# A gate stage's transposes go from TensorE to the DMA, by way of DRAM and as 16-bit halves

## The chip, the cores and the metric

The program runs on one core of one Trainium2 chip. A core has TensorE (PE in the profile; matmuls, and the only engine that could transpose in the kernel before), VectorE (DVE), ScalarE (ACT), GpSimd (POOL), a sync engine (SP) which here only issues DMAs, and 16 DMA engines that all queues share. Each engine executes its instructions in order, so an instruction that waits holds up everything behind it on its engine, and a DMA that waits on SP holds up every DMA behind it on SP. The metric is the device time of one execution in microseconds. The kernel before takes 794.83 us in the median of 3 runs (793.85 to 795.38).

## The reference, cut to what matters

One layer of a trunk, on 512 tokens of width 2048, all in float32:

```python
hn = rmsnorm(x, norm_g[i])
y = swa_mixer(hn, swa_w_in[j], swa_w_out[j], swa_sinks[j], rel_bias)   # ends in (out * silu(gate)) @ w_out
x = x + y
emb = p[i] @ ple_proj[i]
g = jax.nn.sigmoid(rmsnorm(x, ple_norm[i]) @ ple_gate[i])
x = x + emb * g
return rmsnorm(x, final_g)
```

What matters here is the seam between two products: `@ w_out` (the out stage) makes y with tokens on the partitions, x + y is formed in that layout, and `rmsnorm(x) @ ple_gate` (the gate stage) needs x + y once more with its columns on the partitions. Somewhere 512 x 2048 floats have to be transposed.

## The kernel before, in words

Activations of a product are the stationary-side forms with columns on the partitions; weights stream past. To keep float32 accuracy, every float32 operand is split into a high and a low fp32r part, and every product is three matmuls (`mm3`, L124 to L128): high times high, low times high, high times low. Each piece of weights (128 x 1024 floats, 512 KB) is loaded by an SP DMA (L720), cast to its high part by ACT (L727) and subtracted to its low part by DVE (L728).

Each of the two last weighted stages multiplies 2 x 2 blocks by a Winograd scheme, with seven block products instead of eight. The products are numbered 1 to 7; a tuple (`ORDER_OUT`, `ORDER_PLE`) sets the order in which they run. A product has two halves (jj = 0 and 1, the two 512-wide column blocks of its result) of four steps each; a step is one piece of weights and 12 matmuls. In the out stage product 2 is itself done by a smaller Winograd scheme, whose 14 small pieces (6 matmuls each) are put between the steps by the tables `SMALL` and `small_steps`. So the out stage has 62 pieces, numbered 0 to 61, and the gate stage's first product starts with piece 62.

`Forms.steps` makes the four stationary forms of a product: a sum of blocks on DVE where there is one, then a cast on ACT and a subtraction on DVE for each. The blocks of the gate stage are halves of `hT[j]`, the transposed columns 512j to 512j+511 of x + y: product 2 needs columns 1024 to 2047 of the first 256 tokens, product 7 the columns 0 to 1023 of all tokens.

x + y is summed in SBUF as `x1[j][:, t]` (column block j of 512, token block t of 128; 16 tiles) by DVE (`add_to_x`, L1031 and L1033), as the products of the out stage come out of PSUM. When a tile is complete, ACT sums its squares (`squares`, L1001). Then `turn` (L1015) transposes it on TensorE, two column chunks by two token blocks at a time, into a PSUM bank, and ACT copies it out and scales it by the norm's gain (L1018). Of the 16 such turns, 12 stand in the last product of the out stage and 4 in the first product of the gate stage.

What sets the order. The program text sets the order on TensorE and SP throughout. On DVE, ACT and POOL a scheduler sets it from the start of the out stage up to the second product of the gate stage; from there on the program text does. Pieces are prepared ahead: the SP load is placed up to 6 pieces ahead of the piece's use in the out stage (L703 to L720, a ring of 8 buffers from the third product on) and the split two pieces ahead, with three buffers for split pieces, so that ACT can split piece n only when TensorE has finished piece n-3. Products 7, 6 and 4 of the gate stage use weights that are grown in place: loaded once, then another block is added by an accumulating POOL DMA (L707).

The embedding's input `pT` is loaded and split (L1160 to L1162) between the two stages and used from the third product of the gate stage on.

Of the kernel before, what the change touches and what calls it, by code (L numbers as in the profile page):

```python
# [11 lines left out]
F32 = mybir.dt.float32  # L12
F32R = mybir.dt.float32r
AF = mybir.ActivationFunctionType
# [4 lines left out]
D = 2048  # L19
# [36 lines left out]
def trunk_kernel(ctx: ExitStack, tc: tile.TileContext, a: dict):  # L56
# [587 lines left out]
    def blk(t):  # L644
# [4 lines left out]
    ORDER_OUT, ORDER_PLE = (1, 7, 6, 5, 3, 4), (2, 7, 1, 6, 5, 3, 4)  # L649

    SMALL = {
        (5, 0): {1: 1, 3: 1}, (5, 1): {1: 7, 3: 7}, (3, 0): {1: 6, 3: 6}, (3, 1): {1: 2, 3: 2},
        (4, 0): {0: 5, 1: 5, 2: 4, 3: 4}, (4, 1): {0: 3, 1: 3},
# [151 lines left out]
    far_from, far_to = at_out[6, 0][0], at_ple[ORDER_PLE[0], 0][0]  # L805

    class Forms:
# [6 lines left out]
        def steps(self, p):  # L814

            self.made[p] = []
            for h in range(2):
# [3 lines left out]
                if self.nm == "o":  # L821
                    src, sub = {
                        1: (a11, None), 7: (a11, (a21, a11)), 2: (a12, None), 6: (a11, (a22, a11)),
# [7 lines left out]
                if sub:  # L831
                    nc.vector.tensor_sub(src, *sub)
                    yield
# [116 lines left out]
    fg = late.tile([P, D], F32, name="fg")  # L950
    pTh = late.tile([P, 2, S], F32R, name="pTh")
    pTl = late.tile([P, 2, S], F32R, name="pTl")
# [5 lines left out]
    def banks(p, jj, nm):  # L958

        if p in (6, 5, 3):  # L960
            return chain[jj]
        tag = ("to" if p in (7, 2) else "sp")[jj]
        ps = [bank(f"{nm}{p}_{jj}_{tb}", tag) for tb in range(2)]
        if p == 1:
            chain[jj] = ps
        return ps

    later = []
# [6 lines left out]
    def unit(p, jj, at, forms, todo, between=lambda m: None):  # L975

        ps = banks(p, jj, forms.nm)
        f = forms.made[p]
        first = p not in (6, 5, 3)
        for m in range(4):  # L980
            bh, bl = B.get(at[p, jj][m])
            for kk in range(2):
# [22 lines left out]
    def turn(kp, th, tag):  # L1005

        g = kp // 2
        if g not in hT:
            hT[g] = quarter(f"hT{g}")
        tp = bank(f"tp{kp}_{th}", tag)  # L1010
        for n in range(2):
            k = 2 * kp + n
            for tb in range(2):
                src = x1[k // 4][:, 2 * th + tb, (k % 4) * P : (k % 4 + 1) * P]
                nc.tensor.transpose(tp[:, (2 * n + tb) * P : (2 * n + tb + 1) * P], src, ident)  # L1015
        for n in range(2):
            k = 2 * kp + n
            nc.scalar.mul(hT[g][:, k % 4, th * 256 : th * 256 + 256], tp[:, n * 256 : n * 256 + 256], pn[:, k : k + 1])  # L1018

    ple_forms = Forms(hT, "g")  # L1020
    ple_first = ple_forms.steps(2)


    missing = {(j, t): {(0, 0): 1, (1, 0): 3, (0, 1): 1, (1, 1): 2}[t // 2, j // 2] for j in range(4) for t in range(NB)}
# [3 lines left out]
    def add_to_x(j, t, sign, ps):  # L1028
# [6 lines left out]
        if not missing[j, t]:  # L1035
            squares(t, j)

# [4 lines left out]
    small_forms = {}  # L1042

    def small_form(q):
# [5 lines left out]
        fh, fl = (  # L1050
            acts.tile([P, 2, 256], F32R, tag=tag, name=f"small_{tag}{q}").rearrange("p k (h t) -> p (k h) t", h=2)
            for tag in ("ah", "al")
        )
# [16 lines left out]
        (6, 1, 2): 1, (5, 0, 0): 7, (5, 0, 2): 7, (5, 1, 0): 6, (5, 1, 2): 6, (3, 0, 2): 2, (3, 1, 0): 5, (3, 1, 2): 5,  # L1070
        (3, 1, 3): 4, (4, 0, 1): 3, (4, 0, 3): 3,
# [26 lines left out]
    def add_y(p, jj, tb, ps):  # L1098
        c11, c12, c21, c22 = ((2 * v + jj, 2 * u + tb) for u in range(2) for v in range(2))
        whither = {  # L1100
            1: [(c11, -1)], 7: [(c22, 1), (c21, -1)], 6: [(c21, -1)], 5: [(c22, 1)], 3: [(c12, 1)],
# [5 lines left out]
    turns = []  # L1107


# [3 lines left out]
    waiting = {(7, 0): (1, 0), (6, 0): (1, 1)}  # L1113
    held = {}
    for n, p in enumerate(ORDER_OUT):
        nxt = out_forms.steps(ORDER_OUT[n + 1]) if n < 5 else iter(())
        for jj in range(2):
# [11 lines left out]
            def todo():  # L1129
# [5 lines left out]
                if p == 4:  # L1135

                    for _ in range({0: 1, 1: 2, 2: 2, 3: 2, 5: 1, 6: 2, 7: 2}.get(4 * jj + step, 0)):
                        turn(*turns.pop(0), "o")
                    if jj:
                        next(ple_first, None)  # L1140
# [8 lines left out]
        if p == 3:  # L1149
            nc.sync.dma_start(fg, a["final_g"].partition_broadcast(P))  # L1150
        if p == 3:
# [308 lines left out]
```

## Time and profile before

| | us |
|---|---|
| median of 3 runs | 794.83 |
| profiled execution, own time | 794.82 |
| its span | 793.1 |
| out stage, first to last matmul start | 452.3 to 606.4 |
| gate stage, first matmul start | 607.4 |
| TensorE transposes, first to last start | 574.8 to 620.1 |
| busy TensorE / VectorE / ScalarE / GpSimd | 783.2 / 585.7 / 506.7 / 148.5 |

A row of a group of instructions names line, engine, operation, output and inputs, count, and busy time or durations; a row of a stretch gives each engine's busy time in it. Neighbouring matmuls overlap in the profile (each lasts longer than the distance to the next), so what a matmul costs is read from the distance of starts or from the chain of work that ended last, not from its duration. The profiled execution's time is 1.7 us above its span.

### The profile page before, as it was taken

Reading aid. Unit: us, or ns where it says so; the run is one execution under the profiler, and the core shown is the slowest. Engines: PE = TensorE matmul, PEld = TensorE weight load, DVE = VectorE, ACT = ScalarE, POOL = GpSimd, SP = SyncE. Lnnn points to the kernel's source line nnn. Section 1 sums busy time; section 2 is a strip of 40 time slices with the busy share of each in tenths; the row PEclk is TensorE's granted clock in tenths of the full one; section 3 lists DMA queues with packets and bytes.
Section 4 is the critical chain, followed back from the end, with each engine's and each line's share of the span. In section 5 each row is a group of like instructions: output and inputs, shape, how many; then the busy total and the mean of one; then the engine's idle time right before and its main releaser. Section 6 shows DMA issues by size and latency. Waiting matters only on the chain.

```text
span 793.1 us, 11181 instructions
## 1 busy us (share of the span) xinstructions
PE 783.2 (99%) x3746; PEld 656.0 (83%) x3746; DVE 585.7 (74%) x1155; ACT 506.7 (64%) x1067; POOL 148.5 (19%) x248
## 2 busy tenths in 40 slices
PE   9999999999999999999999999999999999999995
PEld 8888888888888888888888888888888888888885
DVE  4547587867867587767777899778866757988896
ACT  6743576666767586766666654466699656656765
POOL 0200423242413324132324200000000120210000
PEclk9999999999999999999999999999999999999998
DMA  9977999897989989898987498667864996787533
GB/s 349 275 215 264 207 275 303 223 267 215 277 227 269 223 249 258 230 247 235 244 227 182 140 365 337 197 212 232 275 237 142 346 203 202 157 225 220 176 107 106
DMA packets 45066, 185.23 MB, mean 234 GB/s; under 512 B 6656, under 2 KB 7680, under 8 KB 39888
## 3 DMA queue, kind: packets, MB, share of 16 engines
q1 hardware_dynamic: 36928, 143.30, 53.0%
q0 software_dynamic: 8080, 41.22, 27.1%
q8 instruction: 29, 0.48, 0.2%
q14 instruction: 29, 0.24, 0.1%
HBM read 177.63 MB, written 62.97 MB: 303 GB/s over the span
## 4 chain that ended last, share of the span: by engine, by line
PE 99%; DVE 0%; ACT 0%; ACTq 0%; issue 0%; DVEq 0%
PE gps L126 7%; PE gps L127 7%; PE gps L128 7%; PE qps L126 7%; PE qps L127 7%; PE qps L128 7%; PE o L127 6%; PE g L128 6%; PE g L127 5%; PE o L126 5%; PE o L128 5%; PE g L126 5%; PE s L477 2%; PE o L583 2%; PE vps L290 2%; PE pt L541 2%
## 5 line engine op out<-in xcount | busy, mean ns | idle before, releaser
L728 DVE TENSOR_TENSOR blo<-braw,bhi 128x1024 fp32r<-128x1024 f32 x102 | 124.4, 1222 | 40.9 <-ACT bhi L727 40.6
L727 ACT CAST bhi<-braw 128x1024 fp32r<-128x1024 f32 x102 | 107.3, 1052 | 72.2 <-PE o L128 24.8
L126 PE MATMUL gps<-xh,whi 128*128 128x512 f32 x256 | 100.0, 390 | 0.0
L127 PE MATMUL gps<-xl,whi 128*128 128x512 f32 x256 | 99.9, 390 | 0.0
L128 PE MATMUL gps<-xh,wlo 128*128 128x512 f32 x256 | 99.8, 390 | 0.0
L126 PE MATMUL qps<-xh,whi 128*128 128x512 f32 x224 | 87.8, 392 | 0.0
L127 PE MATMUL qps<-xl,whi 128*128 128x512 f32 x224 | 87.4, 390 | 0.0
L128 PE MATMUL qps<-xh,wlo 128*128 128x512 f32 x224 | 87.3, 390 | 0.0
L110 DVE TENSOR_TENSOR wlo<-wraw,whi 128x1024 fp32r<-128x1024 f32 x60 | 73.7, 1229 | 6.1 <-ACT whi L109 5.9
L547 DVE TENSOR_TENSOR r<-pt,r 128x256 fp32r<-128x256 f32 x64 | 27.2, 424 | 66.5 <-ACT r L546 65.6
L546 ACT CAST r<-pt 128x256 fp32r<-128x256 f32 x64 | 23.9, 373 | 80.9 <-PE pt L541 80.8
L126 PE MATMUL g<-bhi,fhg 128*128 128x512 f32 x192 | 75.1, 391 | 0.0
L126 PE MATMUL o<-bhi,fho 128*128 128x512 f32 x192 | 74.8, 390 | 0.0
L128 PE MATMUL g<-bhi,flg 128*128 128x512 f32 x192 | 74.8, 389 | 0.0
L127 PE MATMUL o<-blo,fho 128*128 128x512 f32 x192 | 74.8, 389 | 0.0
L128 PE MATMUL o<-bhi,flo 128*128 128x512 f32 x192 | 74.7, 389 | 0.0
L127 PE MATMUL g<-blo,fhg 128*128 128x512 f32 x192 | 74.7, 389 | 0.0
L557 POOL TENSOR_SCALAR_AFFINE_SELECT own<-r 64x512 fp32r<-64x512 f32 (+1 forms) x48 | 32.5, 677 | 224.6 <-DVE r L547 208.7
L109 ACT CAST whi<-wraw 128x1024 fp32r<-128x1024 f32 x60 | 62.2, 1039 | 5.4 <-issue 4.0
L492 POOL COPY t<-sinkb 128x2 f32<-128x2 f32 x64 | 53.2, 839 | 57.7 <-ACT sinkb L873 32.4
L707 POOL DMA_DIRECT2D grown<-in_ple_gate x16 | 13.8, 861 | 231.0 <-DVE blo L728 226.7
L128 PEld LDWEIGHTS gps<-xh,wlo 128*128 128x128 f32 x256 | 48.1, 188 | 10.3
(228 smaller groups left out, 1800.3 us busy)
## 6 DMA issues: line engine op xcount, KB each, us to landing
wraw<-in_w_gate_in SPq DMA_DIRECT2D x32, 512.0 KB, 6.5
w_out<-in_w_out POOLq DMA_DIRECT2D x32, 512.0 KB, 8.0
braw<-w_out SPq DMA_DIRECT2D x32, 512.0 KB, 4.4
wraw<-in_w_q SPq DMA_DIRECT2D x28, 512.0 KB, 5.3
braw<-in_ple_gate SPq DMA_DIRECT2D x24, 512.0 KB, 4.1
braw<-in_w_out SPq DMA_DIRECT2D x22, 512.0 KB, 4.2
xw<-in_first SPq DMA_DIRECT2D x14, 640.5 KB, 6.4
w_out<-in_w_out SPq DMA_DIRECT2D x16, 512.0 KB, 10.1
```

What stands on the lines that cost most here:

```text
L109: nc.scalar.copy(hi, raw)
L110: nc.vector.tensor_sub(lo, raw, hi.bitcast(F32))
L126: nc.tensor.matmul(ps, sh, mh, start=first, stop=False, skip_group_check=more)
L127: nc.tensor.matmul(ps, sh, ml, start=False, stop=False, skip_group_check=more)
L128: nc.tensor.matmul(ps, sl, mh, start=False, stop=last, skip_group_check=more)
L290: nc.tensor.matmul(v_ps[t], h[:, c], part_of(high_at, 256, 512), start=f, stop=e, skip_group_check=True)
L492: nc.gpsimd.tensor_copy(two(0, W + W - 1 if late else W, 1), sinkb[:, d : d + 1].unsqueeze(1).to_broadcast([P, 2, 1]))
L546: nc.scalar.copy(rh, src)
L547: nc.vector.tensor_sub(rl, src, rh.bitcast(F32))
L557: nc.gpsimd.affine_select(out=flat(own), in_=flat(r).bitcast(F32), pattern=[[0, 8], [sign, HB]], compare_op=ALU.is_ge, fill=0.0, base=-HB ...
L727: nc.scalar.copy(hi, raw)
L728: nc.vector.tensor_sub(lo, raw, hi.bitcast(F32))
```

## The change

The transposes leave TensorE. When a tile of x + y is complete, POOL copies it into a buffer with the two 16-bit halves of each float pulled apart (`apart`, L1029 of the changed kernel), and a POOL DMA stores it to DRAM as 128 tokens x 2 halves x 512 columns (L1030). Some steps later SP issues a transposing DMA (L1045) that reads it as 256 rows (token, half) of 512 16-bit values and writes 512 columns of 256 values into `hT[j]`, where the halves lie side by side again as float32. ACT then scales `hT[j]` in place, in SBUF, for pairs of token blocks (L1040). `cross`, called once a step, places the transposing DMA at the fourth call after the store and the scaling at the third call after the second transposing DMA of a pair; `forward` makes the gate stage's forms as far as their input is scaled.

To give this time, the order of products changes: the out stage runs 1, 7, 4, 6, 5, 3 instead of 1, 7, 6, 5, 3, 4 (product 4 now adds to product 7's PSUM banks, so that the sums into x fall by four), and the gate stage starts with product 7 instead of 2. The small products move with it. Their forms, `pT`'s split and the final gain get other buffers.

```diff
-    ORDER_OUT, ORDER_PLE = (1, 7, 6, 5, 3, 4), (2, 7, 1, 6, 5, 3, 4)
+    ORDER_OUT, ORDER_PLE = (1, 7, 4, 6, 5, 3), (7, 2, 1, 6, 5, 3, 4)
...
-    def turn(kp, th, tag):
...
-                nc.tensor.transpose(tp[:, (2 * n + tb) * P : (2 * n + tb + 1) * P], src, ident)
...
+    def apart(t, j):
...
+        nc.gpsimd.tensor_copy(to, x1[j][:, t, :].bitcast(U16).rearrange("p (c h) -> p h c", h=2))
+        nc.gpsimd.dma_start(halves_of[j][t * P : (t + 1) * P], to)
+        written.append((clock[0], t, j))
+
+    def cross():
+
+        clock[0] += 1
+        while crossed and crossed[0][0] <= clock[0] - 3:
+            _, th, j = crossed.pop(0)
+            for k in range(4):
+                part = hT[j][:, k, th * 256 : th * 256 + 256]
+                nc.scalar.mul(part, part, pn[:, 4 * j + k : 4 * j + k + 1])
+            scaled.add((th, j))
+        while written and written[0][0] <= clock[0] - 4:
+            _, t, j = written.pop(0)
...
+            nc.sync.dma_start_transpose(
+                to[:, :, t * 2 * P : (t + 1) * 2 * P], halves_of[j][t * P : (t + 1) * P].rearrange("t h c -> (t h) c")
+            )
...
         if not missing[j, t]:
             squares(t, j)
+            apart(t, j)
...
-        if p == 3:
-            nc.sync.dma_start(fg, a["final_g"].partition_broadcast(P))
-        if p == 3:
-            turns = [(kp, th) for kp0, th in ((4, 1), (4, 0), (0, 0)) for kp in range(kp0, kp0 + 4)]
-    run(ple_first)
+        if p == 5:
+            due(7)
+            fg = late.tile([P, D], F32, tag="two", name="fg")
+            nc.sync.dma_start(fg, a["final_g"].partition_broadcast(P))
+    finish()
...
     nc.sync.dma_start(pT, a["pT"])
+    pTs = late.tile([P, 2, 2, S], F32R, tag="one", name="pTs")
+    pTh, pTl = pTs[:, 0], pTs[:, 1]
```

Three places show how the instructions stand. First SP, at the seam between the stages, before (`braw62` to `braw68` are weights of the gate stage's first product, by piece number; `pT` is the embedding's input):

```order
L720 DMA braw61_6181<-w_out_4_1_3_808 128x1024 [waits DMAHW3_49,DMASW3_49,DVE_49]
L720 DMA braw62_6258<-in_ple_gate 128x1024 [waits DMAHW4_49]
L720 DMA braw63_6270<-in_ple_gate 128x1024 [waits DMAHW5_49,Pool_49]
L720 DMA braw64_6310<-in_ple_gate 128x1024 [waits DMAHW6_49]
L1160 DMA pT_6352<-in_pT 128x1024 [waits DMAHW7_49]
L720 DMA braw65_6361<-in_ple_gate 128x1024 [waits DMAHW7_49,DMAHW0_49,DVE_49]
```

and the same place now (`halves_of2` and `halves_of3` are the DRAM tensors that the POOL DMAs write; DMASW names a wait for such a DMA):

```order
L721 DMA grown67_6295<-ple_gate_7_1_1_814 128x1024 [waits DMAHW5_49,DVE_49]
L1045 DMA_TRANSPOSE hT2_6139<-halves_of2_5009 128x4x256 [waits DMAHW6_49,DMASW2_49]
L1209 DMA pT_6329<-in_pT 128x1024 [waits DMAHW7_49]
L721 DMA grown68_6339<-ple_gate_7_1_2_815 128x1024 [waits DMAHW0_49,DVE_49]
L1045 DMA_TRANSPOSE hT2_6139<-halves_of2_5009 128x4x256 [waits DMAHW1_49,DMASW3_49]
L721 DMA grown69_6363<-ple_gate_7_1_3_816 128x1024 [waits DMAHW2_49,DVE_49]
L1045 DMA_TRANSPOSE hT3_6210<-halves_of3_5010 128x4x256 [waits DMAHW3_49,DMASW6_49,Activation_49]
L721 DMA braw70_6425<-in_ple_gate 128x1024 [waits DMAHW4_49]
L1045 DMA_TRANSPOSE hT3_6210<-halves_of3_5010 128x4x256 [waits DMAHW5_49,DMASW1_49]
```

The load of `pT` now stands behind a transposing DMA, which waits for a store of a tile that the out stage's last product completes in its first half.

Second ACT, around the start of the gate stage (piece 62), before:

```order
L727 CAST bhi60_6228<-braw60_6144 128x1024 [waits DMAHW2_49,PE_49]
L1161 CAST pTh_5006<-pT_6352 128x1024 [waits DMAHW7_49]
L727 CAST bhi61_6260<-braw61_6181 128x1024 [waits DMAHW3_49,DVE_49,PE_49]
L1018 ACTIVATE hT3_6073<-tp7_0_6247,pn_68 128x256 [waits PE_49]
L1018 ACTIVATE hT3_6073<-tp7_0_6247,pn_68 128x256
L844 CAST fhg2_11_6346<-hT3_6073 128x512 [waits Activation_49]
L727 CAST bhi62_6272<-braw62_6258 128x1024 [waits DMAHW4_49,DVE_49,PE_49]
```

and now, in two pieces, at pieces 63 and 64 and at pieces 68 and 69 (`hT3` are columns 1536 to 2047):

```order
L728 CAST bhi63_6297<-grown63_6192 128x1024 [waits DMAHW7_49,DVE_49,PE_49]
L1212 CAST pTs_6331<-pT_6329 128x1024 [waits DMAHW7_49]
L728 CAST bhi64_6341<-grown64_6212 128x1024 [waits DMAHW1_49,DVE_49,PE_49]
...
L728 CAST bhi68_6427<-grown68_6339 128x1024 [waits DMAHW0_49,PE_49]
L1267 COPY s7_6334<-g7_0_1_6338 128x512
L1040 ACTIVATE hT3_6210<-hT3_6210,pn_68 128x256 [waits DMAHW5_49,DMAHW3_49]
L1040 ACTIVATE hT3_6210<-hT3_6210,pn_68 128x256 x2
L728 CAST bhi69_6464<-grown69_6363 128x1024 [waits DMAHW2_49,DVE_49,PE_49]
```

`pT`'s cast moved from ahead of piece 61's cast to ahead of piece 64's, and a scaling that waits for the last two transposing DMAs stands ahead of piece 69's cast.

Third POOL, which before did nothing in the out stage but load x; now, at the end of the out stage (`apart12` is the buffer of the last four tiles; `grown62` to `grown65` are the accumulating DMAs into the weights of pieces 62 to 65):

```order
L1029 COPY apart12_6233<-x1s_5004 128x1024 [waits DMASW4_49,DMASW6_49,DMASW3_49,DVE_49]
L1029 COPY apart12_6233<-x1s_5004 128x1024 [waits DVE_49]
L1030 DMA halves_of2_5009<-apart12_6233 128x1024 [waits Pool_49] x2
L708 DMA grown62_6169<-in_ple_gate 128x1024 [waits DMAHW5_49,DMAHW6_49,DMAHW3_49,DVE_49]
L708 DMA grown63_6192<-in_ple_gate 128x1024 [waits DMAHW4_49,DMAHW0_49,DMAHW7_49,DMASW5_49,DVE_49]
L1029 COPY apart12_6233<-x1s_5004 128x1024 [waits DVE_49]
L1030 DMA halves_of3_5010<-apart12_6233 128x1024 [waits Pool_49]
L708 DMA grown64_6212<-in_ple_gate 128x1024 [waits DMAHW1_49,DMASW7_49,DVE_49]
L1029 COPY apart12_6233<-x1s_5004 128x1024 [waits DVE_49]
L708 DMA grown65_6242<-in_ple_gate 128x1024 [waits DMAHW3_49,DMASW0_49,DVE_49]
L1030 DMA halves_of3_5010<-apart12_6233 128x1024 [waits DMASW1_49,Pool_49]
```

Both copies of a pair stand ahead of the pair's stores for `halves_of2`, and the last store of `halves_of3` stands behind two accumulating DMAs that wait for VectorE to have split pieces 64 and 65.

129 lines of the change are left out of this document (77 added, 52 removed).

## The prediction

> **What bounds the kernel now.** I read the page first (busy shares, chain), then the waits of TensorE, then the transposes, then the chain around the seam of the two stages.
>
> ```profile
> span 793.1 us, 11181 instructions
> PE 783.2 (99%) x3746; PEld 656.0 (83%) x3746; DVE 585.7 (74%) x1155; ACT 506.7 (64%) x1067; POOL 148.5 (19%) x248
> PE 99%; DVE 0%; ACT 0%; ACTq 0%; issue 0%; DVEq 0%
> PE warm_ps L141 <- PEq L1450: 0.8, 1, 0.8
> ```
>
> The chain that ended last is 99% TensorE, and TensorE's only recorded wait is 0.8 us at the start. So each microsecond taken from TensorE is gained, if nothing takes its place; and each wait that TensorE did not have is lost in full.
>
> What a transpose costs is read from the chain (start, length), since single matmuls overlap:
>
> ```profile
> L1015 PE MATMUL tp<-ident,x1s x64: 270/272/273, 574.8 to 620.1; 128*128 128x128 f32 x64
> L1018 ACT ACTIVATE hT<-tp,pn x32: 458/469/492, 576.6 to 621.3; 128x256 f32<-128x256 f32 x32
> 606.75 0.87 PE tp L1015 x8
> 610.37 0.44 PE tp L1015 x4
> ```
>
> Eight hold TensorE for 0.87 us, four for 0.44: 0.109 us each, not the 0.272 of a single record. All 64 are worth 64 x 0.109 = 7.0 us. More cannot be gained on TensorE, since no other matmul goes.
>
> **A clock for the seam.** Where work must be ready follows from these rows:
>
> ```profile
> 480.00:520.00 40.00, 40.00 (x178) 33.11 (x178) 32.85 (x39) 19.97 (x23) 0.00 (x0) 1.00 0.77 272
> L126 PE MATMUL g<-bhi,fhg x192: 389/389/477, 607.4 to 752.9; 128*128 128x512 f32 x192
> ```
>
> 178 matmuls in 40 us are 0.225 us each, 2.70 us a step of 12. The gate stage started at 607.4 behind 48 transposes; without them (5.2 us) it starts at 602.2 on the same clock. From there, if nothing waits: the last out product's first half ends at 591.4 and its second at 602.2; piece 64 begins at 607.6 and piece 69 at 621.1.
>
> **The change part by part.** *Removed*: 64 transposes, -7.0 us. Four sums into x also go from VectorE, and ACT scales from SBUF instead of PSUM (32 scalings before and after); neither engine was on the path: 0.
>
> *Added, on the path from a tile of x to its form*: POOL's copy, POOL's store, the transposing DMA. No row shows the copy's shape, the store or such a transfer. The nearest:
>
> ```profile
> L557 POOL TENSOR_SCALAR_AFFINE_SELECT own<-r x48: 652/660/1584, 104.7 to 448.9; 64x512 fp32r<-64x512 f32 x24, 128x512 fp32r<-128x512 f32 x24
> L1181 POOL DMA_DIRECT2D x1s<-s x4: 856/860/866, 725.7 to 740.2; - x4
> DMA to landing us min/median/max: 4.0/5.2/5.8
> out<-x1s SPq DMA_DIRECT2D x14, 256.0 KB, 2.8
> braw<-in_ple_gate SPq DMA_DIRECT2D x24, 512.0 KB, 4.1
> pT<-in_pT SPq DMA_DIRECT2D x1, 512.0 KB, 9.6
> ```
>
> The copy has the bytes of a 512-column POOL operation (0.66) and twice its elements (1.32); I take 1.3, since the elements are what POOL loops over. The store (256 KB from POOL) I take at the 5.2 of L1181, which has its size and queue, bounds 2.8 and 5.8. The transposing DMA (256 KB on SP) lies between the 2.8 of a quiet 256 KB store and the 9.6 that `pT` took in a burst; I take 3.5, near plain loads.
>
> [...]
>
> *First wait: `pT`.* SP now issues `pT` behind a transposing DMA that waits for the store of a tile finished by the last product's first half (order rows above). Before, the load stood free:
>
> ```profile
> 583.74 0.70 SPq L1160 DMA_DIRECT2D pT<-in_pT  x1
> 597.04 1.05 ACT L1161 CAST pTh<-pT 128x1024 fp32r<-128x1024 f32 x1
> 598.58 1.22 DVE L1162 TENSOR_TENSOR pTl<-pT,pTh 128x1024 fp32r<-128x1024 f32 x1
> 606.79 1.05 ACT L727 CAST bhi<-braw 128x1024 fp32r<-128x1024 f32 x1 [1.11 <-PE o L128]
> L1031 DVE TENSOR_TENSOR x1s<-o,x1s x16: 679/684/692, 485.5 to 606.8; 128x512 f32<-128x512 f32 x16
> ```
>
> Issued 13 us before its cast, it cost nobody anything, though nothing uses it before the third gate product. Now: TensorE is done at 591.4, drained at 591.6; the two sums (0.68 each) end at 592.3 and 593.0; POOL copies both before it stores either: 594.9; the store lands at 594.9 + 5.2 = 600.1; SP issues the transpose and `pT`, 600.5. `pT` lands 4.1 to 9.6 later; among weights, grown blocks and transposes I take 6: 606.5. Behind it ACT holds piece 64's cast. On VectorE, in order: `pT`'s low part (after the cast, 1.05; then 1.22), a sum into x (0.68), piece 64's low part (1.22): 606.5 + 4.2 = 610.7. TensorE wants it at 607.6 + 0.2. **Wait: 2.9 us.** With the low ends (0.66, 4.0, 4.1) the part is ready at 606.3 and there is none; with the high ends (copies 1.3 plus a block of 1.2 each, 5.8, 9.6) it is ready at 617.5: 9.7.
>
> *Second wait: the last pair.* The scheduler put the scaling of the last two tiles, (columns 1536 to 2047, first 256 tokens), ahead of piece 69's cast on ACT. The sum of the first of these two tiles stands behind `pT`'s low part on VectorE, so it ends at 609.4 although TensorE finished the product at 602.2; the second's behind piece 64's low part, at 611.4. POOL: copy to 610.7, store issued to 611.6 (0.86), accumulating DMA for piece 64 to 612.4, copy to 613.7, the DMA for piece 65 (which waits for that piece's split) to 614.6, then the last store: lands at 614.6 + 5.2 = 619.8, transpose at 623.3. ACT then has three scalings (0.47 each), piece 69's cast 1.05, VectorE the low part 1.22: 627.0. TensorE wants it at 621.1 + 0.2 + 2.9 (already late) = 624.2. **Wait: 2.8 us.** Bounds: with the low ends it is ready at 619.9, no wait; with the high ends some 6.
>
> *Third: VectorE and POOL shut each other out.* This row of a two-element copy is the sign:
>
> ```profile
> L492 POOL COPY t<-sinkb x64: 177/1161/1462, 77.5 to 431.0; 128x2 f32<-128x2 f32 x64
> 302.06 1.34 POOL L492 COPY t<-sinkb 128x2 f32<-128x2 f32 x1
> 302.16 1.22 DVE L110 TENSOR_TENSOR wlo<-wraw,whi 128x1024 fp32r<-128x1024 f32 x1
> L110 DVE TENSOR_TENSOR wlo<-wraw,whi x60: 1217/1219/1755, 58.2 to 436.8; 128x1024 fp32r<-128x1024 f32 x60
> 520.00:560.00 40.00, 40.00 (x178) 33.15 (x177) 31.96 (x36) 24.94 (x35) 0.00 (x0) 1.00 0.72 227
> 560.00:575.00 15.00, 15.00 (x69) 12.38 (x68) 12.96 (x16) 9.49 (x13) 0.00 (x0) 1.00 0.83 284
> 575.00:621.00 46.00, 46.00 (x236) 38.54 (x235) 32.47 (x40) 41.02 (x79) 0.00 (x0) 1.00 0.62 218
> ```
>
> Two elements take POOL 0.18 us or 1.16, the length of VectorE's subtraction beside it; and the subtraction, 1.22 in nearly all of 60, once took 1.76, longer by most of a POOL operation. So 16 copies of 1.3 us may take 21 us from VectorE, busy 77.4 of 101 us here (the three stretches). Wholly added, 98.2 would stand against 94 us: 4.2 late; overlapped with VectorE's sums from PSUM, nothing. I take 1.0, a quarter, since a split has some 3 us of slack (two steps, 5.4, less cast and subtraction, 2.3).
>
> [...]
>
> *Moved for nothing*: the order of products (same matmuls); the final gain's load, now also behind a transpose, not needed before the end of the kernel. SP's weight loads in the out stage run up to ten pieces ahead of TensorE (8 buffers), so a transposing DMA that waits there some microseconds eats only that lead.
>
> *Sum*: 793.1 - 7.0 + 2.9 + 2.8 + 1.0 = 792.8 of span; with the 1.7 us around it (own time 794.82) **794.5 us**, against the median of 794.83: no change.
>
> **The rivals.**
>
> *All is hidden.* With the low ends both waits vanish: 794.8 - 7.0 = 787.8. For it: SP's long lead, two to four steps between store and transpose, DMA queues a quarter to a third idle here (share 0.62 to 0.83). Against: the loads now stand in one line behind data that TensorE has only just made, and `pT` cannot start before.
>
> *The transfers are slow (the slower side).* One mechanism: the transposing DMA or its store lands late, and ACT, in order, holds the casts behind the scalings. Its place is ahead of pieces 64 and 69. A store later by d is paid once in the first wait and again in the second; a transpose later by d in the second, and by its traffic in front of `pT` in the first. With 3 us more for each: 794.5 + 3 + 6 = 803, less where slack remains; I put it at 800 (797 to 804). It decides from d of about 1 us, since some 2 us lead from my sum to slower. For it: `pT`'s 9.6 in a burst, and no row of such a transfer. Against: plain 256 KB stores at 2.8.
>
> *VectorE becomes the bound.* 4.2 us in place of 1.0: 797.7. For it: its 80 to 86% in two of the three stretches. Against: 71% in the last, where the late work is.
>
> **How the numbers follow.** What a measurement of this kernel can tell from no change is about 0.2%, 1.6 us: 793.2 to 796.4. The forecast (the waits take most of the gain, 792 to 797): 0.40, of which 0.10 is faster, 0.23 the same, 0.07 slower. All hidden (787.8 to 792): 0.29. Slow transfers: 0.21. VectorE: 0.10. So faster 0.39, same 0.23, slower 0.38. The forecast's own range is 792 to 797; with both signs holding most of the chance the range is 788.0 to 801.0, from all hidden to beyond the middle of the slow case.
>
> **What would show it.** In the changed kernel's waits: TensorE waiting at pieces 64 and 69 for VectorE's low parts, 2 to 4 us each; on ACT the longest waits at the cast of `pT` (for a DMA) and at the scaling of `hT`; `pT` issued near 600 and not at 584; POOL's copies between 1.3 and 2.5 us, VectorE's subtractions beside them lengthened. If TensorE shows no wait there, all is hidden; if it waits earlier too, ahead of scalings in the out stage, or the transposing DMAs take over 6 us, the transfers are slow. The sum is wrong at its root if matmuls ran slower: the granted clock must stay at 1.00.

## The result, and the profile after

The changed kernel takes 819.43 us in the median (814.71 to 822.23), the kernel before on the same chip 794.53 (793.85 to 795.38): slower by 25 us, ratio 1.031, 95% interval 1.026 to 1.036. 794.5 was forecast, and the range ended at 801.0. All times below leave out three executions that lay over 1.5% above the fastest of their kernel, one each of e5 (826.5), e6 (805.0) and e14 (825.9); with them the three medians would be 815.3, 795.6 and 809.4.

The page of the changed kernel: span, busy times, the chain that ended last.

```profile
span 818.2 us, 11139 instructions
PE 785.0 (96%) x3682; PEld 650.2 (79%) x3682; DVE 587.6 (72%) x1151; ACT 507.4 (62%) x1067; POOL 177.9 (22%) x280
PE 81%; DMA 8%; DVE 4%; issue 3%; ACT 2%; POOL 1%; SPq 1%; DVEq 0%; ACTq 0%; POOLq 0%
```

A chain that was 99% TensorE now runs through DMAs for 8% of the span. TensorE does 64 instructions less and is yet busy 1.8 us longer. Its waits, and ACT's for transposed tiles, from the table of waits (total, times, longest, in us; `o` is the out stage, `g` the gate stage):

```profile
PE g L127 <- ACT bhi L728: 10.9, 2, 6.6
PE o L128 <- DVE blo L729: 5.8, 8, 1.2
PE o L127 <- ACT bhi L728: 4.8, 4, 2.0
PE g L128 <- DVE blo L729: 1.3, 3, 0.5
ACT hT L1040 <- DMA hT<-halves_of: 32.0, 7, 11.0
```

TensorE waits 22.8 us in 17 waits: 12.2 in the gate stage, 10.6 already in the out stage (1.25 of them at 472 and 478 us, before the first tile is copied at 534), each time for a weight piece's cast or low part. ACT, which makes the casts, waited 32 us for transposed tiles. The account: TensorE's idle time rises from 9.9 (793.1 - 783.2) to 33.2 us (818.2 - 785.0), +23.3; the transposes are gone, -7.0; so TensorE should be busy 776.2 us and is busy 785.0, +8.8. Together +25.1, the difference of the spans.

The 8.8 us show in the stretches of the changed kernel (length, then PE, PEld, DVE, ACT, POOL busy, granted clock, DMA share, GB/s):

```profile
615.00:620.00 5.00, 5.00 (x24) 4.14 (x23) 1.55 (x2) 1.45 (x3) 1.62 (x2) 1.00 0.94 249
630.00:635.00 5.00, 4.54 (x10) 3.17 (x11) 4.29 (x10) 4.97 (x9) 2.12 (x3) 0.50 1.00 201
650.00:655.00 5.00, 4.06 (x9) 2.89 (x10) 4.19 (x4) 3.23 (x5) 0.85 (x1) 0.50 0.53 140
```

Behind its two long waits TensorE got half its clock: 19 matmuls in 8.6 us where some 38 fit, about 4.3 us lost. The rest fits the restarts. Before a wait the last matmul runs out its whole 0.39 us, where otherwise the next one starts after 0.23; and after a wait of 0.32 to 1.24 us that no second one follows at once, the second matmul starts some 0.33 us behind the first, not 0.23. By my estimate from these that is about 0.26 for each wait, and 17 x 0.26 = 4.4. One of them, and TensorE's wait for piece 64:

```profile
611.15 0.50 PE L128 MATMUL o<-blo,fho 128*128 128x512 f32 x1 [1.24 <-DVE blo L729]
611.48 0.40 PE L129 MATMUL o<-bhi,flo 128*128 128x512 f32 x1
622.69 0.50 PE L128 MATMUL g<-blo,fhg 128*128 128x512 f32 x1 [0.35 <-DVE blo L729]
```

Where the waits come from shows in ACT's timeline at the seam (start, length, and in brackets the idle time before and its cause):

```profile
618.60 1.05 ACT L1212 CAST pTs<-pT 128x1024 fp32r<-128x1024 f32 x1 [3.55 <-DMA pT<-in_pT]
626.84 0.91 ACT L1040 ACTIVATE hT<-hT,pn 128x256 f32<-128x256 f32 x2 [6.25 <-DMA hT<-halves_of]
648.18 1.30 ACT L1040 ACTIVATE hT<-hT,pn 128x256 f32<-128x256 f32 x3 [10.97 <-DMA hT<-halves_of]
```

and in the chain of the same stretch (start, length):

```profile
614.19 4.38 DMA pT<-in_pT
631.79 7.21 DMA halves_of<-apart
640.68 8.62 DMA braw<-in_ple_gate
```

`pT`, forecast to be issued at 600.5 and to land at 606.5, is issued at 614.19 and lands at 618.57. The gate stage starts at 616.5, 14 us behind the forecast's clock, so that TensorE reaches piece 64 late too and waits only 0.35 us there (row above). The scaling of columns 1024 to 1535 stands ahead of piece 65's cast, that of 1536 to 2047 ahead of piece 69's; behind these two TensorE stands 4.3 and 6.6 us. The transposing DMAs as a group (time that the issue takes on SP, min/median/max in ns, first and last start; then from issue to landing in us):

```profile
L1045 SPq DMA_TRANSPOSE hT<-halves_of x16: 1232/1427/3611, 550.6 to 639.0; - x16
DMA to landing us min/median/max: 3.3/6.1/11.5
```

### The profile page after: what moved, and what is told of

The parts are those of the page before. It is cut to its first block, busy times and chain, and to the rows that moved or that the text cites. A ratio compares the mean times of both kernels' runs of the same rounds, so it can differ in the third digit from the quotient of the medians.

```text
span 818.2 us, 11139 instructions
## 1 busy us (share of the span) xinstructions
PE 785.0 (96%) x3682; PEld 650.2 (79%) x3682; DVE 587.6 (72%) x1151; ACT 507.4 (62%) x1067; POOL 177.9 (22%) x280
## 4 chain that ended last, share of the span: by engine, by line
PE 81%; DMA 8%; DVE 4%; issue 3%; ACT 2%; POOL 1%; SPq 1%; DVEq 0%; ACTq 0%; POOLq 0%
PE qps L127 7%; PE qps L128 7%; PE qps L129 7%; PE gps L127 7%; PE gps L128 7%; PE gps L129 7%; PE g L128 5%; PE g L129 5%; PE g L127 5%; DMA halves_of<-apart 3%; PE o L128 2%; PE o L127 2%; PE o L129 2%; PE s L478 2%; DMA hT<-halves_of 2%
## 5 line engine op out<-in xcount | busy, mean ns | idle before, releaser
L729 DVE TENSOR_TENSOR blo<-braw,bhi 128x1024 fp32r<-128x1024 f32 x102 | 127.9, 1258 | 54.4 <-ACT bhi L728 53.8
L127 PE MATMUL g<-bhi,fhg 128*128 128x512 f32 x192 | 76.8, 400 | 10.9 <-ACT bhi L728 10.9
L128 PE MATMUL g<-blo,fhg 128*128 128x512 f32 x192 | 76.6, 399 | 1.3 <-DVE blo L729 1.3
L127 PEld LDWEIGHTS gps<-xh,whi 128*128 128x128 f32 x256 | 48.1, 188 | 9.2
```

The source lines that it names most:

```text
L127: nc.tensor.matmul(ps, sh, mh, start=first, stop=False, skip_group_check=more)
L128: nc.tensor.matmul(ps, sh, ml, start=False, stop=False, skip_group_check=more)
L729: nc.vector.tensor_sub(lo, raw, hi.bitcast(F32))
```

## The experiments

The first theories were T, the transposing transfer itself is slow, and Q, the transfers start late, behind POOL's copies and stores and in order on SP; later W, what is lost is ACT's waiting on late tiles, against D, the traffic itself sets the pace; and, for the traffic without readers, F, the transposing form, against S, SP standing still behind the stores. All are compared with runs of the kernel before on the same chip in the same minutes (794.2 to 794.5).

| | what is tried | median us | ratio, 95% interval |
|---|---|---|---|
| e1 | order of products alone, transposes on TensorE | 795.1 | 1.000 to 1.002 |
| e2 | plain instead of transposing DMAs | 817.8 | 1.025 to 1.031 |
| e3 | transposing DMAs wait for no store | 819.3 | 1.030 to 1.034 |
| e4 | `pT` loaded early | 810.9 | 1.020 to 1.023 |
| e5 | e4, scalings later | 813.0 | 1.022 to 1.028 |
| e6 | e5, last four tiles on TensorE | 795.4 | 1.001 to 1.006 |
| e8 | e1 with `pT` early, and all 16 tiles by DMA, nobody reads them | 809.1 | 1.015 to 1.021 |
| e9 | e8, plain DMAs | 796.6 | 1.002 to 1.004 |
| e10 | e8, transposing DMAs alone | 795.8 | 1.001 to 1.003 |
| e11 | e6, scalings still later | 796.9 | 1.002 to 1.005 |
| e12 | e8, only the last four tiles | 807.1 | 1.010 to 1.021 |
| e13 | eight tiles by DMA, `pT` early | 795.0 | 0.999 to 1.001 |
| e14 | only the last four by DMA, and read | 808.5 | 1.016 to 1.020 |
| e16 | e12, POOL's DMAs do not accumulate | 794.9 | 0.999 to 1.001 |
| e17 | after, POOL's DMAs do not accumulate | 813.8 | 1.022 to 1.026 |
| e18 | e2, POOL's DMAs do not accumulate | 809.4 | 1.017 to 1.020 |

### Is it the DMA path, and which part of it?

**e1.** The new order stays; `apart` and `cross` are replaced by the turns on TensorE.

```diff
-            apart(t, j)
-                cross()
+                if p == 3:
+                    cross({0: 1, 1: 2, 2: 2, 3: 2, 5: 1, 6: 2, 7: 2}.get(4 * jj + step, 0), "o")
```

> The new order of products with the 64 transposes back on TensorE (12 groups of four in the last out product, 4 in the first gate product, scaled by ACT out of PSUM); no copy, store or transposing DMA. If the DMA path makes the loss (theories T and Q alike): 793 to 797, TensorE waits under 2 us in all, as before. If the order of products itself costs (theory O): over 800, with TensorE waiting between 570 and 660 us.

795.14. TensorE waits 0.4 us in all beside its start. So the new order is worth nothing, as forecast, and costs at most 0.9 us (795.14 against 794.20): nearly the whole loss is on the DMA path.

**e2.**

```diff
-            nc.sync.dma_start_transpose(
-                to[:, :, t * 2 * P : (t + 1) * 2 * P], halves_of[j][t * P : (t + 1) * P].rearrange("t h c -> (t h) c")
+            nc.sync.dma_start(
+                to[:, :, t * 2 * P : (t + 1) * 2 * P],
+                halves_of[j][t * P : (t + 1) * P].rearrange("t h (q c) -> t (h q) c", q=2),
             )
```

> As after, but a plain DMA of the same 256 KB takes the place of each transposing one, to the same place, behind the same store, on the same queue (leaves out the transpose: hT holds tokens, not columns, on its partitions; POOL's copy keeps its element count but leaves the bits in place). Theory T (the transposing transfer itself is slow and fills the DMA engines with small packets): most of the 25 us goes, 795 to 802, landing of these transfers 3 to 4 us. Theory Q (the transfers start late, behind POOL's copies and stores and in order on SP; the transposing form adds little): 814 to 820.

817.84, as theory Q had it. The transposing form is not needed for the loss. (POOL's copy and store, not shown in the diff, leave the halves where they lie; the copy then takes 1.53 us in the median instead of 1.22, which works against the plain form a little.) The plain transfers land no sooner (the group, as above):

```profile
L1046 SPq DMA_DIRECT2D hT<-halves_of x16: 530/530/609, 549.8 to 638.3; - x16
DMA to landing us min/median/max: 3.0/6.6/9.1
```

and in its timeline ACT stands at two of the same places, `pT` and the last pair:

```profile
620.88 1.04 ACT L1214 CAST pTs<-pT 128x1024 fp32r<-128x1024 f32 x1 [11.24 <-DMA pT<-in_pT]
646.65 1.70 ACT L1041 ACTIVATE hT<-hT,pn 128x256 f32<-128x256 f32 x4 [11.91 <-DMA hT<-halves_of]
```

**e3.**

```diff
-                ..., halves_of[j][t * P : (t + 1) * P].rearrange("t h c -> (t h) c")
+                ..., zeros_of[0 : 2 * P]
```

> As after, but each transposing DMA reads 256 KB of zeros that lie in DRAM since the start of the out stage, so none waits for a store; copies and stores stay (leaves out the real transpose: hT is zero). Theory T: the same transfers at the same places in SP's queue, so the loss stays, 810 to 820, landing median still 6 us, DMA share still 1.0 or more between 550 and 650 us. Theory Q: the chain copy, store, wait is gone: 790 to 800.

819.27, as theory T had it. Two experiments, each right for the other theory: either the two causes are each enough, or both theories are wrong. The trace shows the first. The two waits of 6 and 11 us are gone, and one of 23.4 us stands in their place, behind a transposing DMA whose issue alone held SP for 14 us. SP's timeline:

```profile
610.10 14.09 SPq L1049 DMA_TRANSPOSE hT<-zeros_of  x1
```

and ACT's:

```profile
643.14 1.30 ACT L1044 ACTIVATE hT<-hT,pn 128x256 f32<-128x256 f32 x3 [23.39 <-DMA hT<-zeros_of]
```

Without its store to wait for, it went out among POOL's accumulating DMAs (from 606.30 on), and the DMA engines, nearly all busy (share 1.31 from 600 to 620 us), fell to 20 to 60 GB/s from 611.5 to 620 us. The e8 group below follows that up.

**e4.** `pT` is loaded at the end of product 6, not between the stages.

```diff
+        if p == 6:
+            nc.sync.dma_start(pT, a["pT"])
```

> As after, but pT is loaded during the second half of the out stage, ahead of the transposing DMAs (SP row 200 of 286, not 231). If SP's order in front of pT matters as forecast: TensorE's wait at piece 64 goes, 3 to 6 us faster than after (813 to 816). If the pieces behind are late by their own transfers: within 2 us of after.

810.9, 8.5 us faster than after, but not as expected: the wait at piece 64 did not go. With `pT` out of the way ACT meets the scaling of columns 1024 to 1535 already ahead of piece 64's cast, and waits 15.8 us there, TensorE 11.2 (tables of waits):

```profile
PE g L127 <- ACT bhi L728: 11.2, 1, 11.2
ACT hT L1040 <- DMA hT<-halves_of: 26.1, 6, 15.8
```

TensorE waits 11.7 us in the gate stage, where it waited 12.2. What is saved lies in the out stage, 5.0 us of waits instead of 10.6, and in one stretch at half clock instead of two: TensorE is busy 781.9 us instead of 785.0. That the early `pT` shortened the out stage's waits is not shown: e17 below has ACT's casts and scalings of the out stage in the same order as after, and waits only 5.9 us there.

**e5.**

```diff
-        while crossed and crossed[0][0] <= clock[0] - 3:
+        while crossed and crossed[0][0] <= clock[0] - 6:
```

> As e4 (pT early), and the scalings of a pair of tiles stand six steps behind their transposing DMAs instead of three, so that ACT meets them later: the last pair's behind piece 72's cast and not piece 69's. Theory W (what is lost is waiting of ACT, in order, on transfers that land late; the transfers' traffic by itself is cheap): TensorE's 11.2 us wait in the gate stage goes to under 3, and the run to 794 to 800. Theory D (the DMA engines and the VectorE/POOL lock set the pace, whoever waits): TensorE waits elsewhere instead, 806 to 812 as e4.

812.98: nothing is won. ACT waits half as long for the tiles as in e4 (26.1 us), and now for weights (table of waits):

```profile
ACT bhi L728 <- DMA braw<-in_ple_gate: 14.9, 3, 8.5
ACT hT L1040 <- DMA hT<-halves_of: 13.1, 5, 5.8
```

On SP the weight loads stand behind the transposing DMAs; the chain runs through a store of 6.15 us, its transposing DMA's issue at 621.55, the next one's at 623.76 (4.05) and then a weight load that lands after 13.99. A wait taken off ACT's order comes back by SP's order.

### Which tiles?

**e6.** From e5; the tiles that the last out product finishes go back to TensorE.

```diff
-            apart(t, j)
+            if t // 2 or j < 2:
+                apart(t, j)
+            else:
+                turns.append((t, j))
```

> As e5, and the four tiles that the last out product finishes (columns 1024 to 2047, first 256 tokens) go over TensorE again in the first gate product (16 transposes, 1.7 us); 12 tiles go by DMA. Theory W: the late transfers are gone, no TensorE wait over 1 us in the gate stage; 48 transposes saved are 5.2 us: 789 to 795. Theory D: 12 transposing DMAs still press the out stage, TensorE still waits there some 5 us: 797 to 805.

795.38 (792.8 to 797.7): 17.6 us of e5 go with four of sixteen tiles. Between the theories: the gate stage has no wait left, as W had it, but the 5.2 us of saved transposes are not won, as D had it. (Its profiled execution is its fastest, with 2.2 us of waits in the out stage.)

**e14** is its complement: only these four by DMA, `pT` late as in after.

```diff
+            if t < 2 <= j:
+                apart(t, j)
```

> The complement of e6: only the last four tiles (columns 1024 to 2047, first 256 tokens) go by DMA and are read, pT stands behind them as in after, 48 transposes stay on TensorE. If the loss of after is made by these four: 812 to 822, TensorE waiting in the gate stage alone. If the twelve earlier ones have a share of their own, in the out stage: 803 to 811.

808.54, below the 812 of the first theory: the four make 14 us of the loss, not all. Most of it is one wait of TensorE (table of waits):

```profile
PE g L127 <- ACT bhi L728: 10.5, 1, 10.5
```

and one transposing DMA took SP 8.3 us to issue amid POOL's accumulating ones; the scaling behind it on ACT waited 11.9. SP's timeline, and ACT's:

```profile
618.75 8.34 SPq L1062 DMA_TRANSPOSE hT<-halves_of  x1
```

```profile
627.51 1.30 ACT L1057 ACTIVATE hT<-hT,pn 128x256 f32<-128x256 f32 x3 [11.88 <-DMA hT<-halves_of]
```

So the twelve earlier tiles alone cost 1.2 us net (e6), the last four alone 14.1, all sixteen 24.9, or 18.8 in e5. These do not add up, and they can't be set against each other strictly, since e5 and e6 load `pT` early and scale later, and e14 does not. A likely reason, which no run isolates: the twelve delay the out stage by waits in front of the casts, and SP has twelve transposing DMAs more between its weight loads.

**e11 and e13** look for what is left to win. e11 moves e6's scalings back further. e13 sends only the tiles of the last 256 tokens by DMA: half of them are finished early, the other half read late.

```diff
# e11
+        for at in [v for v in crossed if v[0] <= clock[0] - (8 if v[2] < 2 else 14)]:
# e13
-            if t // 2 or j < 2:
+            if t // 2:
```

> As e6 (12 tiles by DMA, the last four on TensorE; 795.6, its profiled execution 792.8 with 2.2 us of TensorE waits in the out stage, where ACT waited 8.8 us for transposed tiles), with the scalings of columns 0 to 1023 eight steps behind their transposing DMAs and those of columns 1024 to 2047, last 256 tokens, fourteen, in the gate stage, where nothing needs them yet. If ACT's in-order waits make what is left of the loss: 789 to 793. If the traffic in the out stage does: 794 to 797.

> pT early; only the eight tiles of the last 256 tokens go by DMA (32 transposes, 3.5 us, off TensorE); columns 0 to 1023 of these are finished by about 555 us and scaled in the last out product, columns 1024 to 2047 are finished by 586 and needed only by the fourth gate product, and scaled in the gate stage. The other eight go over TensorE, four in the last out product, four in the first gate product. If only the late tiles and ACT's early meeting of transposed ones cost: 795.1 - 3.5 = 791 to 793, below the kernel before. If eight transposing DMAs press the out stage as twelve do: 794 to 797.

796.91 and 795.03. e11 is no better than e6, with TensorE waiting 5.0 us in the out stage. In e13's profiled execution (792.5, its fastest) TensorE is busy 779.7 us, 3.5 less than before, just the price of 32 transposes, with 1.2 us of waits; the other ten runs lie between 793.5 and 795.6. Over all runs the ratio is 1.0002: eight tiles by DMA are no loss and no gain that can be measured. No version that beats the kernel before was found.

### The traffic without its readers

**e8.** e1, and beside it all copies, stores and transposing DMAs, which land in the room that the copy came from.

```diff
-            nc.sync.dma_start_transpose(
-                to[:, :, t * 2 * P : (t + 1) * 2 * P], ...
+            nc.sync.dma_start_transpose(
+                slots.pop(0).rearrange("p (k t) -> p k t", k=4), ...
```

> As e1 (new order of products, all 64 transposes on TensorE; 795.1), with pT early, plus all 16 copies, stores and transposing DMAs in their old places, but nothing reads what they bring (they land in the room that the copy came from). It is the traffic without the dependence. Theory W: 794 to 797. Theory D: over 800, TensorE waiting between 550 and 660 us for casts and low parts whose weights land late; the slowed clock after each wait adds to it.

809.13, as theory D had it, but not by its mechanism. TensorE waits only 0.3 us in the out stage; the loss is one wait of 12.1 us at 638.5, for a weight piece. SP's timeline:

```profile
612.42 0.68 SPq L721 DMA_DIRECT2D grown<-ple_gate  x1
613.21 16.07 SPq L1059 DMA_TRANSPOSE apart<-halves_of  x1
```

and the chain:

```profile
612.42 24.90 DMA grown<-ple_gate
```

A transposing DMA that takes 16 us to issue, and a weight load of 512 KB, issued just ahead of it, that takes 24.9 to land. **e9, e10, e12 and e16** take this apart: the form, the transposing DMAs without copy and store, the last four tiles only, and these four beside POOL DMAs that do not accumulate.

```diff
# e9
-            nc.sync.dma_start_transpose(
+            nc.sync.dma_start(
# e10: apart() without its copy and store, and
-                to, halves_of[j][t * P : (t + 1) * P].rearrange("t h c -> (t h) c")
+                to, zeros_of[0 : 2 * P]
# e12
+            if t < 2 <= j:
                 apart(t, j)
# e16: e12, and
-                nc.gpsimd.dma_start(t, src, accum_op=ALU.add)
+                nc.gpsimd.dma_start(t, src)
```

> As e8 (809.1: all copies, stores and transposing DMAs, nobody reads them), but plain DMAs of the same bytes at the same places of SP's queue. Theory F (the transposing form: its issue held SP for up to 16 us in e8, median 2.0 against 0.5 for a plain DMA, and the weight load behind it landed 25 us late): most of the 15 us goes, 794 to 798, no issue on SP over 3 us. Theory S (SP stands still behind the stores, so the weight loads go out late whatever the form): 804 to 810.

> As e8, but without copies and stores: 16 transposing DMAs of zeros that lie in DRAM, at the same places of SP's queue, waiting for no store, read by nobody. Theory F: those that meet POOL's accumulating DMAs after 605 us are held or hold SP for 10 us or more, as in e3, 800 to 812. Theory S: nothing waits, 794 to 797.

> As e8, but only the last four tiles (columns 1024 to 2047, first 256 tokens) are copied, stored and transposed by DMA; 12 of 16 do nothing. If the loss of e8 is made where these four meet POOL's accumulating DMAs and SP's loads for the gate stage: 802 to 810. If it is the sum of sixteen: under 799.

> As e12 (the last four tiles copied, stored and transposed by DMA, read by nobody; 807.1), but POOL's eight DMAs for the gate stage's grown blocks load plainly, without adding to what lies in SBUF (leaves out those sums: the third gate product's weights are wrong). If transposing DMAs and accumulating DMAs in flight together slow each other: 794 to 798, no landing over 12 us. If the transposing DMAs slow the DMA engines whatever else runs: 803 to 810, the DMA engines still under 150 GB/s between 620 and 640 us.

796.60, 795.79, 807.14 and 794.88. Where nobody reads, the loss needs the transposing form (e9 has no loss) and accumulation (e16 has none), and the last four tiles are enough for nearly all of it (e12; its four runs lie at 802 to 803 and at 811 to 812, so the collision is not the same each time). In e10 the last transposing DMA went out at 603.4, before POOL's accumulating ones (603.8 on), so the two hardly met; theory F expected a loss there and was wrong on that, theory S was wrong on e9. The stretch from 620 to 640 us, of e12 and then of e16 (length, then PE, PEld, DVE, ACT, POOL busy, clock, DMA share, GB/s):

```profile
620.00:640.00 20.00, 13.78 (x61) 10.93 (x60) 4.37 (x5) 4.57 (x7) 2.26 (x3) 0.91 1.25 129
```

```profile
620.00:640.00 20.00, 20.00 (x92) 16.62 (x91) 11.60 (x12) 12.15 (x18) 1.59 (x3) 1.00 1.00 303
```

With accumulation the engines are full at 129 GB/s, without it they are full at 303. The slowest landing among the four transposing DMAs is 25.1 us in the one and 7.8 in the other, and e12's weight load issued at 621.33 took 25.29. All versions of this group load `pT` early. Plain DMAs that are read with `pT` early were not run, so e9 against e2 does not tell the reading from `pT`'s place.

### The same with readers

**e17** takes accumulation out of the changed kernel, **e18** out of e2 (the one-line edit of e16).

> The changed kernel as it is, all 16 tiles by DMA and read, but POOL's eight DMAs for the grown blocks load plainly (leaves out those sums: the third gate product's weights are wrong). If the meeting of transposing and accumulating DMAs makes the loss here as it does where nobody reads (e12 to e16: 807 to 795): 795 to 803. If the chain of late transfers in front of ACT's casts makes it by itself: 810 to 820.

> As e2 (plain DMAs in place of the transposing ones, read; 817.8), and POOL's eight DMAs load plainly as in e17. Neither form that could disturb the other is left; what is left is the chain copy, store, transfer, pT, scaling, cast in its order. If that chain makes the loss: 808 to 818. If accumulating DMAs slow the stores and transfers of the chain: 795 to 803.

813.80 and 809.41. Both lie where the chain makes the loss by itself. With plain DMAs and nothing that accumulates, the chain alone is 14.3 us above e1. What is left of the loss is shared by two things, and the shares depend on which is taken away first: accumulation 5.6 us (819.4 to 813.8) or, with plain DMAs, 8.4 (817.8 to 809.4); the transposing form 1.6 (819.4 to 817.8) or, without accumulation, 4.4 (813.8 to 809.4). The 1.6 can't be told from nothing, since the runs of after lie between 814.7 and 822.2. Nor are the 5.6 clearly accumulation's: of the 8.1 us between the spans of the two profiled executions 4.7 are waits in the out stage, all of them before POOL's first DMA for the grown blocks (614.9 in after, 609.2 in e17). With plain DMAs it is clearer: the gate stage's waits fall from 16.6 to 10.0 us. So accumulating DMAs delay the chain even where its form is plain; where the tiles are not read, only the transposing form costs time (809.1 in e8, 796.6 in e9). In the changed kernel itself SP never stands long on a transposing DMA (3.6 us at most, above). TensorE's waits in e18:

```profile
PE g L127 <- ACT bhi L728: 8.3, 2, 4.4
PE o L128 <- DVE blo L729: 3.6, 5, 1.6
PE g L128 <- DVE blo L729: 1.7, 2, 1.3
```

and the two waits of ACT behind most of them, in its timeline:

```profile
616.61 1.04 ACT L1214 CAST pTs<-pT 128x1024 fp32r<-128x1024 f32 x1 [9.40 <-DMA pT<-in_pT]
637.73 1.70 ACT L1041 ACTIVATE hT<-hT,pn 128x256 f32<-128x256 f32 x4 [7.74 <-DMA hT<-halves_of]
```

## Why the prediction was wrong, point by point

**The step that failed** is the sum's price of the path, read as two short waits in front of pieces 64 and 69 (2.9 and 2.8 us) behind transfers of 3.5 us, with nothing lost before. The kind of wait was right: ACT, in order, held the casts behind `pT` and behind the scalings of late tiles. In the changed kernel one of the two places was right, neither size was, and three terms were missing:

| us of span | forecast | changed kernel |
|---|---|---|
| transposes | -7.0 | -7.0 |
| waits in the out stage | 0 | 10.6 |
| wait at piece 64 | 2.9 | 0.35 |
| wait at piece 65 | 0 | 4.7 |
| wait at piece 69 | 2.8 | 7.1 |
| matmuls at half clock, and restarts | 0 | 8.8 |
| VectorE and POOL | 1.0 | within the waits |

- *Transposes, -7.0*: holds as far as it can be seen. e13 shows 3.5 us less busy TensorE for 32 of them.
- *Transposing DMA, 3.5 us*, my choice between 2.8 and 9.6: it landed after 6.1 in the median and 11.5 at most. I had put it near a quiet 256 KB store; the row nearest in its surroundings was `pT`'s 9.6 in a burst. It has nothing to do with the form: plain DMAs landed after 6.6 in the same place (e2). I had also read the free share of the DMA engines off the kernel before. With the stores and the transfers back there is none left; the same stretch (last numbers: DMA share, GB/s) before and after:

```profile
580.00:600.00 20.00, 20.00 (x102) 16.75 (x101) 15.16 (x17) 18.24 (x35) 0.00 (x0) 1.00 0.47 165
580.00:600.00 20.00, 17.23 (x73) 13.13 (x71) 10.34 (x10) 11.47 (x25) 5.62 (x6) 1.00 1.07 275
```

- *First wait, 2.9*: 0.35 in the changed kernel. `pT` was 12 us late, as the store that gates it was, but the out stage ran 14 us behind, so TensorE came late as well. With plain DMAs, where the out stage lost less, the wait was there and dearer: 8.1 in e2, and 5.7 in e18 (4.4 at the cast's reader, 1.3 at the low part's). Loading `pT` early (e4) gave back 8.5 us, but TensorE then waited 11.6 at this piece for a scaling.
- *Second wait, 2.8*: 7.1 in the changed kernel (6.6 and 0.5), 4.3 in e18 (3.84 at 640.42, 0.47 at 641.68 in its TensorE timeline). The last store stood on POOL behind an accumulating DMA which waits for a split, as the forecast said, and the store took 7.2 instead of 5.2.
- *A pair left out*: columns 1024 to 1535 in front of piece 65. By the forecast's own clock its transposing DMAs were in by about 605 (600.5, the issue beside `pT`, and 3.5) and needed no term; they held ACT for 6.25 us up to 626.84 and TensorE for 4.7 (4.26 and 0.46 in its timeline).
- *Nothing in the out stage*: it lost 10.6 us there in the profiled execution, and 5.9 in e17's. I looked only at the seam; the scheduler put scalings of early tiles in front of casts too, and they met transfers of 6 to 9 us.
- *SP's weight loads, moved for nothing*: wrong at the seam, where the lead is used up. In e5 and e12 ACT waits for weights that were issued behind a transposing DMA.
- *VectorE and POOL, 1.0*: not contradicted. The copies took 1.39 us in the mean, 1.3 were forecast; VectorE's 102 splits of loaded weights took 127.9 us instead of 124.4. In the timelines of the changed kernel a copy (1024 elements of 16 bits) took 1.05 us with VectorE nearly idle (at 575.86) and 1.97 beside a subtraction (621.57), and a subtraction 2.05 beside a copy (609.04) where 1.22 is usual; a sum from PSUM took 0.68 beside a copy (622.56) as elsewhere. With all copies and stores, plain DMAs and no reader (e9) the kernel is 1.5 us above e1, which is this price and the traffic's together.
- *The clock must stay at 1.00*: it did not, and some 4.3 us of the loss are that, with about as much at restarts. The forecast named the sign, but had no term for it.

Of the rivals, "the transfers are slow" (800, 797 to 804) comes nearest: its signs (transposing DMAs over 6 us, TensorE waiting earlier) came true, and one of its two places. It priced a delay of 3 us twice; what it lacked was that each delay moves the next store and transfer too, that SP's weights stand in the same line, and what TensorE pays after standing still (the 8.8 of the table). The bounds failed with it: "high ends" of 9.7 and 6 were taken for each wait alone, and the range should have reached at least their sum with the third term's 4.2; even that, 786.1 + 9.7 + 6 + 4.2 + 1.7 = 807.7, lies 12 us short.

Whether a transposing DMA is as fast as a plain one has three answers in these runs. To landing it was (6.1 against 6.6 us in the median, after and e2); in its issue it was not (1.23 us on SP at least, against 0.53 in e2); and beside accumulating DMAs it was not (up to 25.1 us to landing in e12, against 7.8 without accumulation in e16 and 10.0 for plain ones in e9). The rival had 0.21, and the transfers of the changed kernel were slow for another reason than their form.

What stays open: why the out stage's waits differ so much with casts and scalings in the same order (10.6 in after, 5.9 in e17); what `pT`'s place alone is worth, since e4 moved other waits with it; why one and the same accumulating load slows a transposing DMA and is slowed by it, and how much of the changed kernel's out-stage waits comes from the twelve transposing DMAs' share of the engines rather than from ACT's order. e8 has the same transfers in the out stage with 0.3 us of waits, which speaks for ACT's order.

## What to carry to other kernels

A detour through DRAM is a chain of four queues (copy, store, load back, use), and each of them that ran in order held unrelated work behind the late item (ACT stood 10.97 us at one scaling, piece 69's cast behind it); so price the chain at its busiest moment, with transfer times from bursts, and follow every in-order queue on it, not only the last. Move to DMA only what is finished long before it is read: here 12 of 16 tiles went over almost without loss, though without the 5.2 us of gain too, and the last four cost 14 us alone. TensorE, which otherwise never stopped, paid more for its waits than their length (8.8 us beside 22.8), and taking a wait out of one queue won nothing while the next one held the same work (e4 to e5, 810.9 to 813.0).

## What the runs showed of the hardware

*Transposing and accumulating DMAs in flight together slowed each other and the weight loads beside them.* e12 against e16: 129 GB/s instead of 303 with full DMA engines (620 to 640 us), a landing of a transposing DMA of up to 25.1 us instead of 7.8, SP's weight loads landing after 25.4 us in the median instead of 6.9 (600 to 640 us), the first gate product's eight POOL DMAs landing after 17.3 us in the median instead of 7.0 (or 9.6, accumulating beside plain DMAs, e9), a transposing DMA's issue on SP of up to 16.07 us (e8), where it took 1.23 to 1.35 without accumulation (e16).

*What TensorE paid after a wait.* In e8, behind its one long wait of 12.07 us (chain of waits; start and length of single matmuls):

```profile
639.77 0.80 PE g L128
640.57 0.43 PE g L129
640.99 0.43 PE g L127
...
644.41 0.43 PE g L129
644.83 0.25 PE g L127
645.08 0.24 PE g L128
645.32 0.23 PE g L129
```

For 5 us each matmul takes 0.43 instead of 0.23, and TensorE is busy 786.7 us where e1 with the same matmuls has 783.3: 3.4 us, nearly all for one wait. In the changed kernel the waits of 4.26 and 6.63 us were followed by such a stretch (0.50 above); the longest of the out stage, 2.01 us and one matmul later 0.76, was not. In the profiled executions each of the 13 waits between 3.84 (e18) and 21.7 us (e3) was followed by one, but shorter waits were too: 3.2 us in e5, and in e11 1.76 and 0.76 us with one matmul between them (TensorE's timeline; the granted clock from 580 to 590 us is 0.83):

```profile
582.52 0.50 PE L127 MATMUL o<-bhi,fho 128*128 128x512 f32 x1 [1.76 <-ACT bhi L728]
583.78 0.66 PE L128 MATMUL o<-blo,fho 128*128 128x512 f32 x1 [0.76 <-DVE blo L729]
584.24 0.63 PE L129 MATMUL o<-bhi,flo 128*128 128x512 f32 x1
```

So the length of the wait alone did not decide it: 2.01 and 0.76 us in the changed kernel cost no such stretch, 1.76 and 0.76 in e11 did. What decides is not shown.
